# One output store of a mixture-of-experts kernel, put as five transfers in place of one

## The chip, the cores and the metric

The kernel runs on one core of a Trainium2 chip. The metric is the device time of one execution in microseconds (us). The core has a matrix engine (TensorE, PE in the profile), three engines that work on vectors (VectorE or DVE, ScalarE or ACT, GpSimd or POOL), a synchronisation engine (SyncE or SP) that here only issues transfers, and 16 DMA engines that all transfers between the chip's memory (HBM) and the core's on-chip memory (SBUF) share. A transfer is issued by GpSimd (queue q0 in the profile, called the ring here), by SP (q1) or by ScalarE (q10).

## The reference

Eight experts, each a two-layer network on its own 256 tokens:

```python
n_experts, capacity, hidden, expert_hidden = 8, 256, 512, 2048
h = np.matmul(x, w1) + b1[:, np.newaxis, :]
h = np.maximum(h, 0)
return (np.matmul(h, w2) + b2[:, np.newaxis, :]).astype(np.float32)
```

All inputs and the output are float32. The weights alone are 64 MB in HBM, the output is 4 MB.

## The kernel before

Tokens, hidden rows and expert rows are cut to the 128 partitions of SBUF. For each expert the weights are loaded by GpSimd, which converts them to fp16 on the way (`load_w1` L82, `load_w2` L88); x is loaded, for later experts in groups (`load_x` L72), and transposed in 32 x 32 blocks by VectorE (`transposes` L95). `first_product` (L114) makes relu(x w1 + b1) in PSUM and writes it as fp16 with ScalarE; `second_product` (L166) multiplies by w2, three experts later (LAG = 3), and calls `store`.

`store` (L142) copies the two halves of the result from PSUM to SBUF, one by VectorE (L156), one by ScalarE (L157). What follows depends on the expert. Experts 0 to 3 and experts 4 and 5 are groups (`GROUPS = {0: 4, 4: 2}`, L36): their results are gathered in one tile, 16 KB or 8 KB per partition, and only noted in `pending` when the last expert of the group is done. Expert 6 is stored at once in three parts (`PARTS`, L40): 25 rows by SP, 96 by ScalarE's queue, 7 by SP. Expert 7 is stored at once as 128 rows by SP (L164).

The order of GpSimd's transfers is written out by hand: `ring` (L215 to L225) is a list of (step, function, arguments), worked off from its head at the start of each step of the last loop (L227 to L234). The weights of the last experts come first, and then `flush` (L138) for the group of experts 0 to 3 and for the group of experts 4 and 5, so that these two stores, 2 MB and 1 MB, stand last in the ring. `ordered` keeps GpSimd's instructions in program order. The transfers of the ring signal on eight counters that are used in turn, and a transfer that takes a counter waits, where the program cannot tell it in another way, until the one before it on that counter has landed. At the end of the program SP waits for all counters, and a barrier over all engines closes it.

Of the kernel before, what the change touches and what calls it, by code (L numbers as in the profile page):

```python
# [10 lines left out]
def kernel(  # L11
# [9 lines left out]
    nc = tc.nc  # L21
# [16 lines left out]


    PARTS = {E - 2: ((0, 25, False), (25, 121, True), (121, 128, False))}  # L40
    nXF32 = 2
    X_LOADS = {2: 2, 4: 4}

    def ordered(ins):
        return tc.keep_in_program_order(ins)
# [91 lines left out]

    def flush(first):  # L138
        dst, src = pending.pop(first)
        ordered(nc.gpsimd.dma_start(out=dst, in_=src))  # L140

    def store(e, po):  # L142
        if e in group_of:
# [15 lines left out]
        if e in group_of:  # L159
            if e == first + n - 1:  # L160
                pending[first] = (dst, out_sb)
            return
        for p0, p1, scalar in PARTS.get(e, ((0, P, False),)):
            (nc.scalar if scalar else nc.sync).dma_start(out=dst[p0:p1], in_=out_sb[p0:p1])  # L164
# [23 lines left out]
    for e in range(nXF32):  # L188
# [4 lines left out]
        out=b2_sb,  # L193
        in_=b2.rearrange("e h -> (e h)").rearrange("(o f) -> o f", o=1),
# [12 lines left out]
    for b in range(nB):  # L207
        nc.vector.transpose(  # L208
            out=b1T[b * B : (b + 1) * B, nB - 1 - b : nB - 1 - b + nJ * B],
            in_=b1_rows.rearrange("r (i j) -> r j i", j=nJ),  # L210
# [13 lines left out]
    for first, n in GROUPS.items():  # L224
        ring.append((first + n + LAG, flush, (first,)))  # L225
# [40 lines left out]
```

## Time and profile before

| | |
|---|---|
| Time, median of 3 runs | 181.69 us (181.60 to 181.88) |
| Span of the profiled execution, first to last instruction | 179.7 us |
| DMA, read from and written to HBM | 71.39 MB and 4.19 MB, 421 GB/s over the span |
| PE busy (matrix products) | 129.1 us, 72% |
| DVE, ACT, POOL busy | 88.0, 70.2 and 13.1 us |
| Store of experts 0 to 3 (ring, 2 MB) | issued 148.26, 26.8 us to landing |
| Store of experts 4 and 5 (ring, 1 MB) | issued 159.71, 17.8 us to landing |
| Store of expert 7 (SP, 512 KB) | issued 173.94, 4.8 us to landing |

The profile is of one execution; times in it are counted from the start of its span, and no time of that execution beyond the span is given. A store lands when its last packet is confirmed. The trace has a record of every DMA packet with its start, duration, queue and size, but not with the DMA engine that moved it; a packet of 4 bytes is the one with which a DMA engine reports that its share of a transfer is done.

### The profile page before, as it was taken

How to read it: one execution, taken by the hardware profiler on the slowest of the kernel's cores; microseconds unless marked ns; L12 is line 12 of the kernel's file. 1: busy time of each engine (PE TensorE's matmuls, PEld its weight loads, DVE VectorE, ACT ScalarE, POOL GpSimd, SP SyncE). 2: the span in 40 equal slices, each digit the busy share in tenths (PEclk: the TensorE clock that was granted, in tenths of full speed). 3: DMA queues.
4: the chain of work that ended last, by engine and by line, in shares of the span. 5: the costliest groups of instructions: out<-in, count | busy, mean ns of one | idle time of the engine just before them, and what ended most of it. 6: DMA issues, size and time to landing. Idle time of an engine off the chain costs nothing.

```text
span 179.7 us, 1958 instructions
## 1 busy us (share of the span) xinstructions
PE 129.1 (72%) x784; PEld 85.8 (48%) x784; DVE 88.0 (49%) x125; ACT 70.2 (39%) x151; POOL 13.1 (7%) x28
## 2 busy tenths in 40 slices
PE   0005099969595970899969597969497887999950
PEld 0004079969592320795369244844195332433420
DVE  0999942987000199999999998003200020301010
ACT  0000459969593022483099005950586020020010
POOL 7000002120201010001010001000200021010000
PEclk9999999999998798589999889999999996999996
DMA  5999999999999999999999999999999999999996
GB/s 216 251 226 199 233 212 197 233 224 193 228 230 192 221 233 215 197 230 230 204 208 230 219 193 233 226 193 222 230 215 197 233 206 204 223 212 215 335 420 250
DMA packets 3829, 40.56 MB, mean 226 GB/s; under 512 B 461, under 2 KB 477, under 8 KB 1133
## 3 DMA queue, kind: packets, MB, share of 16 engines
q0 software_dynamic: 3232, 38.35, 96.6%
q1 hardware_dynamic: 476, 1.70, 2.4%
q10 hardware_dynamic: 112, 0.39, 0.5%
q8 instruction: 6, 0.10, 0.2%
q14 instruction: 3, 0.02, 0.0%
HBM read 71.39 MB, written 4.19 MB: 421 GB/s over the span
## 4 chain that ended last, share of the span: by engine, by line
DMA 66%; PE 26%; POOL 2%; another core or an unknown queue 1%; issue 1%; ACT 0%; POOLq 0%
DMA w1sb<-in_w_dram 44%; DMA w2sb<-in_w_dram 22%; PE po L178 18%; PE ph L121 8%; PE po L171 1%; POOL w1sb L84 1%; ACT out L157 0%; POOL x L76 0%; POOL b_sb L192 0%; POOL b_rows L196 0%; POOLq L250 0%
## 5 line engine op out<-in xcount | busy, mean ns | idle before, releaser
L121 PE MATMUL ph<-xT,w1sb 128*128 128x256 f16 x512 | 63.6, 289 | 34.8 <-DMA w1sb<-in_w_dram 23.9
L121 PEld LDWEIGHTS <-w1sb 128*128 128x128 f16 x512 | 59.0, 147 | 40.3 <-DMA w1sb<-in_w_dram 32.6
L178 PE MATMUL po<-w2sb,hT 128*128 128x512 f16 x256 | 61.4, 402 | 9.4 <-DMA w2sb<-in_w_dram 9.4
L112 DVE STREAM_TRANSPOSE xT<-x 32x256 f16<-32x256 f16 (+1 forms) x64 | 53.1, 889 | 25.6 <-DMA x<-in_x_dram 18.7
L128 ACT ACTIVATE hT<-ph,b1T 128x256 f16<-128x256 f32 x128 | 56.2, 474 | 13.6 <-PE ph L121 13.4
L178 PEld LDWEIGHTS <-hT 128*128 128x128 f16 x256 | 25.9, 102 | 44.7 <-issue 19.3
L156 DVE COPY out<-po 32x512 f32<-32x512 f32 (+2 forms) x22 | 15.1, 688 | 54.0 <-PE po L178 53.8
L157 ACT COPY out<-po 32x512 f32<-32x512 f32 (+2 forms) x22 | 12.7, 579 | 69.7 <-PE po L178 69.5
L109 DVE STREAM_TRANSPOSE xT<-x 32x256 f16<-32x256 f16 x32 | 14.0, 436 | 0.5
L93 POOL DMA_DIRECT2D w2sb<-in_w_dram x10 | 5.3, 534 | 72.8 <-PE po L178 72.8
L128 ACT ACT_TABLE_LOAD x1 | 1.3, 1283 | 20.5 <-DVE b1T L208 20.5
L84 POOL DMA_DIRECT2D w1sb<-in_w_dram x8 | 4.5, 558 | 63.2 <-PE ph L121 62.4
L171 PE MATMUL po<-b_sb,ones 1*128 1x512 f16 x16 | 4.8, 379 | 0.0
L208 DVE STREAM_TRANSPOSE b1T<-b_rows 32x512 f32<-32x512 f32 x4 | 4.1, 1035 | 0.1
L201 DVE CAST x<-x 128x1024 f16<-128x1024 f32 x2 | 1.5, 757 | 3.3 <-DMA x<-in_x_dram 3.3
L140 POOL DMA_DIRECT2D out_dram<-out x2 | 1.1, 542 | 10.9 <-ACT out L157 10.9
L171 PEld LDWEIGHTS <-ones 1*128 1x128 f16 x16 | 0.9, 92 | 2.1 <-issue 2.1
L76 POOL DMA_DIRECT2D x<-in_x_dram x2 | 1.1, 552 | 0.0
L197 DVE MEMSET ones<- 1x128 f16 x1 | 0.2, 165 | 0.8 <-PEq L250 0.8
L196 POOL DMA_DIRECT2D b_rows<-in_b_dram x1 | 0.5, 515 | 0.0
L192 POOL DMA_DIRECT2D b_sb<-in_b_dram x1 | 0.5, 513 | 0.0
L250 POOL MEMSET const-float32-0.0<- 128x1 f32 x1 | 0.1, 99 | 0.2 <-issue 0.2
(3 smaller groups left out, 0.3 us busy)
## 6 DMA issues: line engine op xcount, KB each, us to landing
w1sb<-in_w_dram POOLq DMA_DIRECT2D x8, 2048.0 KB, 34.5
w2sb<-in_w_dram POOLq DMA_DIRECT2D x6, 2048.0 KB, 46.8
w2sb<-in_w_dram POOLq DMA_DIRECT2D x4, 1024.0 KB, 24.0
out_dram<-out POOLq DMA_DIRECT2D x1, 2048.0 KB, 26.8
x<-in_x_dram SPq DMA_DIRECT2D x2, 512.0 KB, 3.9
x<-in_x_dram POOLq DMA_DIRECT2D x1, 1024.0 KB, 30.8
out_dram<-out POOLq DMA_DIRECT2D x1, 1024.0 KB, 17.8
x<-in_x_dram POOLq DMA_DIRECT2D x1, 512.0 KB, 24.0
```

The costliest lines, as they stand in the source:

```text
L84: ordered(nc.gpsimd.dma_start(out=w1_sb[e], in_=w1[e].rearrange("(p kc) m -> p kc m", kc=nKC)))
L93: ordered(nc.gpsimd.dma_start(out=w2_sb[e][:, lo : lo + half], in_=src[:, lo : lo + half]))
L109: nc.vector.transpose(out=out[:, :, g, :, 0, :], in_=block[:, :, :, 0, :])
L112: nc.vector.transpose(out=out[:, tb, g], in_=block[:, tb])
L121: ordered(nc.tensor.matmul(out=ph, lhsT=w1_sb[e][:, kc, :].rearrange("p (q j) -> p q j", j=nJ)[:, :, j], rhs=xT[e][:, kc, :], start=(kc == 0),
L128: nc.scalar.activation(out=hT[e][:, j, :].rearrange("p (tb k i) -> p tb k i", tb=nTB, k=split), in_=ph.rearrange("p (tb i k) -> p tb k i", ...
L156: nc.vector.tensor_copy(out=out_sb[at : at + rows, k * nTB, :], in_=po[0][part])
L157: nc.scalar.copy(out=out_sb[at : at + rows, k * nTB + 1, :], in_=po[1][part])
L171: ordered(nc.tensor.matmul(out=t, lhsT=ones1, rhs=b2_sb[0:1, e * H : (e + 1) * H], start=True, stop=False,))
L178: ordered(nc.tensor.matmul(out=po[tb], lhsT=hT[e][:, j, tb * P : (tb + 1) * P], rhs=w2_sb[e][:, j, :], start=False, stop=(j == nJ - 1),))
L201: nc.vector.tensor_copy(out=t, in_=x32[e])
L208: nc.vector.transpose(out=b1T[b * B : (b + 1) * B, nB - 1 - b : nB - 1 - b + nJ * B], in_=b1_rows.rearrange("r (i j) -> r j i", j=nJ),)
```

## The change

The store of experts 4 and 5 is a tile of 128 rows of 8 KB. Before, GpSimd puts it in the ring as one transfer. After, GpSimd puts the rows 0 to 65, 66 to 90, 91 to 101 and 102 to 126 as four transfers in this order, with the limit of 4096 bytes to a descriptor, so that a row is two runs of 4 KB; the last row, 127, is issued by SP, with a limit of 512.

```diff
     PARTS = {E - 2: ((0, 25, False), (25, 121, True), (121, 128, False))}
+    RING_PARTS = {4: ((0, 66), (66, 91), (91, 102), (102, 127))}
     nXF32 = 2
...
     def flush(first):
         dst, src = pending.pop(first)
-        ordered(nc.gpsimd.dma_start(out=dst, in_=src))
+        if first not in RING_PARTS:
+            ordered(nc.gpsimd.dma_start(out=dst, in_=src))
+            return
+        for p0, p1 in RING_PARTS[first]:
+            ordered(nc.gpsimd.dma_start(out=dst[p0:p1], in_=src[p0:p1], max_dma_last_dim=4096))
+        nc.sync.dma_start(out=dst[p1:], in_=src[p1:], max_dma_last_dim=512)
```

In the built program GpSimd has 30 instructions of note in place of 27, and SP 8 in place of 7: the one-row store stands after the two loads of x and before the stores of expert 6. The instructions of the other engines and their order are the same. The third and the fourth of the ring's parts wait for a counter of the ring each.

## The prediction, made before the run

> **What bounds the kernel now.** I read the slices of the span first (busy share of the 16 DMA engines in tenths, and what they moved), then the queues (packets, MB, share of 16 engines' time):
>
> ```profile
> DMA  5999999999999999999999999999999999999996
> GB/s 216 251 226 199 233 212 197 233 224 193 228 230 192 221 233 215 197 230 230 204 208 230 219 193 233 226 193 222 230 215 197 233 206 204 223 212 215 335 420 250
> ...
> q0 software_dynamic: 3232, 38.35, 96.6%
> q1 hardware_dynamic: 476, 1.70, 2.4%
> q10 hardware_dynamic: 112, 0.39, 0.5%
> q8 instruction: 6, 0.10, 0.2%
> ```
>
> The DMA engines are the bound from the first slice to the last; GpSimd's ring (q0) holds 96.6% of their time, SP's queue is q1, ScalarE's q10. In the last three slices only stores are left. The chain of waits (start, length, what) breaks off too early:
>
> ```profile
> 166.28 7.03 PE po L178 x32
> 173.31 0.02 issue
> 173.33 0.59 ACT out L157
> ```
>
> It ends at 173.92 us of 179.7, because nobody computes on what a store writes. So I read the store issues (KB, us to landing) and the end of the timeline (start, length, engine, line):
>
> ```profile
> out_dram<-out POOLq DMA_DIRECT2D x1, 2048.0 KB, 26.8
> ...
> out_dram<-out POOLq DMA_DIRECT2D x1, 1024.0 KB, 17.8
> ...
> out_dram<-out SPq DMA_DIRECT2D x1, 512.0 KB, 4.8
> ```
>
> ```profile
> 148.26 0.55 POOL L140 DMA_DIRECT2D out_dram<-out  x1
> 159.71 0.54 POOL L140 DMA_DIRECT2D out_dram<-out  x1 [10.90 <-ACT out L157]
> ```
>
> The changed store is the 1024 KB one, put in the ring at 159.71 and landed 17.8 us later, because loads and the 2 MB store are ahead of it. The last, expert 7's 512 KB by SP, is issued at 173.94 and lands at 178.78. The last 2 us, in half-microsecond windows (length, engines, clock, DMA share, GB/s):
>
> ```profile
> 177.00:177.50 0.50, 0.00 (x0) 0.00 (x0) 0.00 (x0) 0.00 (x0) 0.00 (x0) 0.50 0.93 377
> 177.50:178.00 0.50, 0.00 (x0) 0.00 (x0) 0.00 (x0) 0.00 (x0) 0.00 (x0) 0.50 0.70 287
> 178.00:178.50 0.50, 0.00 (x0) 0.00 (x0) 0.00 (x0) 0.00 (x0) 0.00 (x0) 0.50 0.27 107
> ```
>
> The share falls in steps: some engines are done a microsecond before others. The packet records (start, duration, queue, size) name no engine, but from 161.5 us on they lie end to end in exactly sixteen chains, none with a gap over 4 ns, each with 8 rows of each 128-row transfer. Five chains end at 177.04, 177.33, 177.38, 177.44 and 177.55; eleven at 178.07 to 178.43; the mean is 177.99. Five of the eleven, the SP chains from here on, are those that carry 5 rows each of SP's 25-row store; two more are the rest of the seven that its 7-row store used (25 rows left 5 completion packets, 7 rows left 7). The other four late ones carry no more rows than the early five. The q8 line says why they can be late: six instruction fetches of 16 KB, 0.9 to 1.0 us each, and six chains run about 1 us behind. The last packet, at 178.43, lands at 178.78, and SP's end waits and the closing barrier take until 179.7. A chain that ends late is the kernel's time, one for one.
>
> **The change part by part.** The sum is made against the profiled span, 179.7 us; the median of the runs is 181.69, 2.0 us more, which lies around the span and which I leave alone.
>
> *Issues on GpSimd.* Three more at 0.54 us: 1.6 us, so the four end at about 161.9 instead of 160.25. Nothing is queued behind them on GpSimd. Two carry new waits on ring counters whose transfers had landed by 149.50 and 154.42. The ring reaches this store at 173.02 at the earliest: 11 us of cover, cost nothing; without it, 1.6 us.
>
> *Order on SP.* The one-row store waits for expert 5's ScalarE copies (end 159.4) ahead of expert 6's stores, issued at 166.40. SP is idle in between, an issue takes 0.36 us: nothing. SP's end waits stay eight.
>
> *4 KB descriptors.* An 8 KB ring store packet starts 307 ns after the one before it, a 4 KB store packet on q1 and q10 155 ns (256 records). No ring store has 4 KB packets in this trace; I take 155. Two for one costs 3 ns per row, 0.03 us on a chain.
>
> *More pieces.* Each ends with a completion packet, 6 ns from start to start: three more are 0.02 us. [...] In this trace a chain goes from one ring transfer to the next within 10 ns, so the row decides.
>
> *Where the rows go.* This carries the sum, and the trace does not show it: all its ring transfers divide by sixteen. The nearest rows are SP's: 25 rows went to five engines, 5 each, 7 to seven, 1 each. By that, 66 rows are 11 engines x 6, 25 are 5 x 5, 11 are 11 x 1, 25 are 5 x 5. If each part starts where the one before stopped, sixteen engines are gone round twice: eleven get 7 rows, five get 10. If each starts at the first engine, as SP's two did, five get 17, six get 7, five none. I take the first: the instruction queue's fetches fell on six different chains, so a queue that moves on exists here; this is the weakest step. [...]
>
> With 7 rows a chain gets 14 x 155 + 18 - 8 x 307 = -0.27 us; with 10 rows 20 x 155 + 18 - 8 x 307 = +0.66 us. If the five are the early chains: 177.55 + 0.66 = 178.21, and the late 178.43 - 0.27 = 178.16. The end moves from 178.43 to 178.21: -0.22 us.
>
> *SP's one row.* The built program has it as one run of 2048 elements, while the ring parts show as rows of two 1024s: its limit of 512 has not cut it. One row on SP's queue goes by the row of 25 and 7 to one engine, and to one they also used: an SP chain, 0.31 us. Those end at 177.80 to 178.15 after the change; with the row at 178.11 to 178.46. Cut into sixteenths it costs each chain some 0.03 us, between a 4-byte and a 4 KB packet. So the end lies between 178.21 and 178.46, -0.22 to +0.03; over the five possible chains the mean is 178.34, which I take: -0.1 us. It also holds up one chain's loads by 0.31 us; those chains' loads land by 168.3, the slowest land at 169.23, and TensorE asks for them at 169.68.
>
> Forecast: 181.69 - 0.10 = **181.59 us**, own range 181.40 to 181.80 (-0.22 and +0.03, and the before runs' own scatter of 0.1 to 0.2).
>
> **The rivals.**
> 1. *The 25-row parts fall on late chains* (the ring's count starts elsewhere, or all sixteen are used with 10 rows on eleven). For: nothing in the trace ties the ring's order to the early five. Against: five and eleven are also the numbers of early and late chains. It decides as soon as one late chain takes 10 rows: 178.43 + 0.66 = 179.09; with SP's row on it 179.40; and if the ring's last landing is then the very last, SP has three more end waits of 0.06 behind it. +0.65 to +1.15: about 182.5 us, slower.
> 2. *Every part starts at the first engine.* SP's stores speak for it. Then an SP chain has 17 rows: 34 x 155 + 18 - 2456 = +2.83 us, 178.42 to 181.25: 184.5 us.
> 3. *The row on SP is spread after all, or falls on a light chain*, and the balance comes through whole: -0.2 us, 181.48. Against it stands the uncut run. The gain is capped: were all chains to end together, at the mean 177.99 plus 0.05, it would be 0.39 us, 181.30.
>
> A measurement of this kernel tells about 0.2% (0.36 us) from no change, so my own mechanism is mostly too small to be told.
>
> **How the numbers follow.** Forecast 0.42, rival 3 0.18, rival 1 0.32, rival 2 0.08. Faster by over 0.2% needs nearly the whole cap; most of that chance is in rival 3: 0.18. Within 0.2%: the forecast and the rest of rival 3, 0.42. Slower: rivals 1 and 2, 0.40. The range goes from 181.35 to 182.60: it takes in the forecast, most of rivals 3 and 1, and leaves out rival 2.
>
> **What would show it.** DMA share in the last half microseconds: above 0.9 until close to 178 and then a steep fall if balanced; if rival 1 holds, a longer low tail than now, with q0 packets past 177.2. The number of 4-byte packets on q0 and the chain each 25-row part stands on show the split; an 8192-byte q1 packet near 160 us shows SP's row uncut. If late chains do not end about 0.27 us earlier, the split is wrong; if they do and the end stays, SP's row or a wait behind the ring's landing holds it.

## The result, and the profile after

The changed kernel takes 183.08 us (median of 6 runs, 182.53 to 183.54); the kernel before took 181.73 us beside it (6 runs, 181.50 to 182.01). The ratio is 1.0075, 95% interval 1.0060 to 1.0089: slower by 0.75%, 1.35 us between the medians. Medians and ratios here and below are of fast runs; one run of all, 272.43 us in e3, was slow and stands in neither. The profiled execution after took 182.94 us, its span is 181.1 us against 179.7.

The slices of the span of the changed kernel (busy share of the 16 DMA engines in tenths, and what they moved), then its queues:

```profile
DMA  6998999999899989998999999999999999999994
GB/s 231 232 232 190 232 232 203 206 226 232 186 228 201 248 192 224 228 217 192 232 224 213 199 232 224 210 203 232 224 206 206 228 201 210 226 208 210 403 371 166
...
q0 software_dynamic: 3696, 38.34, 96.3%
q1 hardware_dynamic: 478, 1.71, 2.5%
```

Up to the last three slices both kernels move 186 to 251 GB/s in every slice. In those three it was 335, 420 and 250 GB/s before and is 403, 371 and 166 now. (The slices are 4.5 us long and no longer begin at the same moments, so only their run is compared.) The ring's queue has 464 packets more.

The chain of waits of the changed kernel (start, length, what) ends where it ended before, 0.3 us later, and the store of expert 7 follows it:

```profile
169.98 3.63 PE po L184 x16
173.63 0.59 ACT out L163
```

The issues of stores (KB, us to landing) and the line of the issues in the timeline (start, length):

```profile
out_dram<-out POOLq DMA_DIRECT2D x1, 2048.0 KB, 27.4
...
out_dram<-out POOLq DMA_DIRECT2D x1, 528.0 KB, 19.8
...
out_dram<-out SPq DMA_DIRECT2D x1, 512.0 KB, 6.0
out_dram<-out POOLq DMA_DIRECT2D x2, 200.0 KB, 19.2
...
out_dram<-out POOLq DMA_DIRECT2D x1, 88.0 KB, 19.4
```

```profile
158.14 2.59 POOL L145 DMA_DIRECT2D out_dram<-out  x4 [9.31 <-ACT out L163]
```

The four issues take 2.59 us in all. The ring's parts land about 19 to 20 us after they were issued, and the store of expert 7, which the change does not touch, now takes 6.0 us in place of 4.8.

The end in windows (start to end, length, five engines, clock, share of the DMA engines' time, GB/s), before and then after:

```profile
174.00:177.00 3.00, 0.00 (x0) 0.00 (x0) 0.00 (x0) 0.00 (x0) 0.00 (x0) 0.95 0.96 401
177.00:178.00 1.00, 0.00 (x0) 0.00 (x0) 0.00 (x0) 0.00 (x0) 0.00 (x0) 0.50 0.81 332
178.00:179.00 1.00, 0.00 (x0) 0.00 (x0) 0.00 (x0) 0.00 (x0) 0.00 (x0) 0.50 0.14 53
```

```profile
174.00:177.00 3.00, 0.00 (x0) 0.00 (x0) 0.00 (x0) 0.21 (x1) 0.00 (x0) 1.00 0.99 342
177.00:178.00 1.00, 0.00 (x0) 0.00 (x0) 0.00 (x0) 0.00 (x0) 0.00 (x0) 1.00 0.90 275
178.00:179.00 1.00, 0.00 (x0) 0.00 (x0) 0.00 (x0) 0.00 (x0) 0.00 (x0) 1.00 0.77 299
179.00:180.00 1.00, 0.00 (x0) 0.00 (x0) 0.00 (x0) 0.00 (x0) 0.00 (x0) 0.50 0.17 70
```

This is the reading that matters. From 174 to 177 us the share went up, from 0.96 to 0.99, and the rate went down, from 401 to 342 GB/s. The engines are not idle for want of work, and work that is badly dealt out would not lower the rate at a full share: packets take longer. The packet records say so too. Before, all 128 packets of this store took 309 to 318 ns. After, 37 of its 254 ring packets of 4 KB took over 175 ns where the others took 159, up to 899 ns, 8.6 us too much in all. SP's 4 KB packets of expert 7's store have lost 0.8 us and the last 16 KB ones 1.2 us beside them. So 10.6 us of engine time, 0.66 us on each of 16 engines, went into slow packets, plus 290 packets of 4 bytes, 9 ns each for most and 7 for some (2.6 us at 9 ns, 0.16 us on each). The mean end of the sixteen chains rose from 177.99 to 179.00 us, so that these two make 0.8 of the 1.0 us; the rest is open.

That the store of expert 7 was issued 0.3 us later is not the cause: among the runs below, e12 issued it at 174.06 us and lost nothing, and e4 at 173.65, the earliest of all, and is among the slowest.

### The profile page after: what moved, and what is told of

It is laid out like the page before. It is cut to its first block, busy times and chain, and to the rows that moved or that the text cites. A ratio compares the mean times of both kernels' runs of the same rounds, so it can differ in the third digit from the quotient of the medians.

```text
span 181.1 us, 1963 instructions
## 1 busy us (share of the span) xinstructions
PE 126.6 (70%) x784; PEld 86.0 (47%) x784; DVE 87.9 (49%) x125; ACT 70.5 (39%) x151; POOL 15.3 (8%) x31
## 4 chain that ended last, share of the span: by engine, by line
DMA 60%; PE 19%; DVE 9%; issue 6%; ACT 1%; POOL 0%; another core or an unknown queue 0%; POOLq 0%; ACTq 0%
DMA w1sb<-in_w_dram 46%; PE ph L122 13%; DMA w2sb<-in_w_dram 12%; PE po L184 6%; DVE xT L110 6%; DVE b1T L214 2%; DMA x<-in_x_dram 2%; DVE x L207 1%; ACT L129 1%; ACT out L163 0%; PE po L177 0%; ACT hT L129 0%; POOL w2sb L94 0%; POOLq L85 0%
## 5 line engine op out<-in xcount | busy, mean ns | idle before, releaser
L122 PE MATMUL ph<-xT,w1sb 128*128 128x256 f16 x512 | 65.8, 296 | 38.6 <-DMA w1sb<-in_w_dram 27.0
L122 PEld LDWEIGHTS <-w1sb 128*128 128x128 f16 x512 | 60.4, 148 | 44.9 <-DMA w1sb<-in_w_dram 37.2
L184 PE MATMUL po<-w2sb,hT 128*128 128x512 f16 x256 | 56.7, 379 | 8.3 <-DMA w2sb<-in_w_dram 8.3
L184 PEld LDWEIGHTS <-hT 128*128 128x128 f16 x256 | 24.7, 98 | 40.1 <-issue 11.9
L145 POOL DMA_DIRECT2D out_dram<-out x4 | 2.6, 652 | 9.3 <-ACT out L163 9.3
L142 POOL DMA_DIRECT2D out_dram<-out x1 | 0.5, 543 | 0.0
```

The costliest lines, as they stand in the source:

```text
L122: ordered(nc.tensor.matmul(out=ph, lhsT=w1_sb[e][:, kc, :].rearrange("p (q j) -> p q j", j=nJ)[:, :, j], rhs=xT[e][:, kc, :], start=(kc == 0),
L184: ordered(nc.tensor.matmul(out=po[tb], lhsT=hT[e][:, j, tb * P : (tb + 1) * P], rhs=w2_sb[e][:, j, :], start=False, stop=(j == nJ - 1),))
```

## The experiments

Two theories stood first. By the *place* theory the rows of the new parts lie on the wrong engines: late chains take 10 rows, and packets go at their normal pace. By the *crowding* theory something in the new transfers slows the packets: their 4 KB size, their number, the packets of 4 bytes, or the stretch of partitions that each covers. Every run changes only this store, unless said otherwise. The table gives the median, the ratio to the kernel before on the same chip, and the packets of this store in the ring that took over a tenth more than their nominal 159 ns (4 KB) or 309 ns (8 KB), with the time that these lost in all. The code below is shortened to the lines that matter (`...` marks a gap).

| run | store of experts 4 and 5 | median us | ratio, 95% interval | slow packets | lost us |
|---|---|---|---|---|---|
| e1_again | as changed | 183.29 (one run) | | 48 of 254 | 10.2 |
| e2_shift2 | as changed, another load cut | 184.39 | 1.0148 (1.0106 to 1.0190) | 24 of 254 | 7.2 |
| e3_neutral | 55, 25, 48 rows, 4 KB | 184.08 | 1.0123 (1.0100 to 1.0147) | 64 of 256 | 16.9 |
| e4_k16 | 48, 32, 16, 32 rows, 4 KB | 184.33 | 1.0151 (1.0129 to 1.0174) | 95 of 256 | 23.8 |
| e5_one4k | 128 rows at once, 4 KB | 181.62 | 1.0000 (0.9980 to 1.0019) | 0 of 256 | 0 |
| e6_no4k | as changed, 8 KB | 184.38 | 1.0149 (1.0131 to 1.0168) | 36 of 127 | 16.8 |
| e7_halves | 64 and 64 rows, 8 KB | 183.92 | 1.0124 (1.0106 to 1.0142) | 38 of 128 | 13.4 |
| e8_cols | 128 rows, columns in halves | 181.63 | 1.0002 (0.9980 to 1.0024) | 0 of 256 | 0 |
| e9_shift_true | as changed, another load cut | 184.68 | 1.0165 (1.0134 to 1.0196) | 54 of 254 | 14.2 |
| e10_sbuf_half | two transfers from 64 partitions each, all over HBM | 183.51 | 1.0096 (1.0078 to 1.0113) | 76 of 256 | 11.9 |
| e11_hbm_half | two transfers from 128 partitions, HBM in two blocks | 181.82 | 1.0009 (0.9997 to 1.0021) | 0 of 256 | 0 |
| e12_every_other | 64 even rows, 64 odd rows, 8 KB | 181.65 | 1.0003 (0.9980 to 1.0026) | 0 of 128 | 0 |

**The change once more, and with its place shifted.** The first is the changed kernel itself. The second cuts an early load of 32 rows, so that the ring's count of engines should begin elsewhere. The *divisor rule* of the expectations is the author's estimate from SP's stores of before, where 25 rows went to five engines and 7 to seven: a part goes to as many engines as the largest number up to 16 that divides its rows.

```diff
-    ordered(nc.gpsimd.dma_start(out=b1_rows, in_=b1.rearrange("e (b i) -> (e b) i", b=nB)))
+    b1_src = b1.rearrange("e (b i) -> (e b) i", b=nB)
+    for p0, p1 in ((0, 28), (28, 32)):
+        ordered(nc.gpsimd.dma_start(out=b1_rows[p0:p1], in_=b1_src[p0:p1]))   # e2; e9 adds max_dma_last_dim=1024
```

> The changed kernel once more, for a second profile. Three terms are under suspicion for its +1.4 us. Place: the ring's 25-row parts (10 rows per engine) stand on five engines of which two are among the six late ones, +0.66 us. Bursts: an engine that has no row of a part gets as many 4-byte packets as the others get data packets (290 in all), and data packets beside such bursts are slow, +0.8 us. Pieces: 4 KB descriptors and four transfers cost more in themselves. If the starting engine of the ring's count is fixed, this profile shows again three early and two late chains with 4-byte packets at the place of the 66-row part, and about 183.0 us. If the count is left over from what ran before, another number of late chains, and a time between 181.5 and 183.5.

> The changed kernel, with the load of b1 put as 28 and 4 rows in place of 32, which by the divisor rule moves the ring's count on by 14 + 4 = 18, two engines past where it was. Place: if the count starts anew in each execution, the 25-row parts now stand on the five early chains, and the time falls by about 0.66 us, to some 182.4 (to 181.6 if place is all). If the count is carried over, it moves on by two in each execution and the times spread over 181.6 to 183.5. Bursts and pieces: no gain from the shift, 183.0 to 183.2.

The first gave 183.29 us and 48 slow packets: the crowding belongs to the change, not to one execution. The second gave 184.39 us, above what either theory had (183.5 at most), and the 66-row part ended early on the same classes of engines as in the changed kernel, three early chains and two later ones. Whether the count was shifted can't be told from that, and the run does not separate the theories. Its ring lands at 180.84 us, later than in the changed kernel (179.17), with fewer slow packets; why is open.

**The same number of rows for each engine.** By the divisor rule 55 rows are 11 engines x 5, 25 are 5 x 5 and 48 are 16 x 3, so every engine gets 8 rows as before. The second run uses only multiples of 16. Neither has SP's row.

```diff
-    RING_PARTS = {4: ((0, 66), (66, 91), (91, 102), (102, 127))}
+    RING_PARTS = {4: ((0, 55), (55, 80), (80, 128))}             # e3
+    RING_PARTS = {4: ((0, 48), (48, 80), (80, 96), (96, 128))}   # e4
```

> The ring store as 55, 25 and 48 rows in 4 KB descriptors, no row by SP: every engine gets 5 + 3 rows again, wherever the count starts, but 160 of the 4-byte packets stay. Place: as before, 181.7 to 181.8. Bursts: about half of 0.8 us, 182.0 to 182.5. Pieces: about 182.5 to 183.

> The ring store as 48, 32, 16 and 32 rows in 4 KB descriptors, no row by SP: four pieces and 4 KB as in the changed kernel, but all divide by sixteen, so no 4-byte packets beyond the completions and 8 rows on each engine. Place and bursts: as before, 181.7 to 181.9. Pieces: 183.0.

Both are slower than the changed kernel, 1.0123 and 1.0151, with no row misplaced by that rule, and slower than any theory had them (183.0 at most). The ring's packets fit the rule in e3: 3552 are before's 3232, 128 more of data, 32 completions and 160 of 4 bytes for engines without a share. The windows of e3 and of e4:

```profile
174.00:177.00 3.00, 0.00 (x0) 0.00 (x0) 0.00 (x0) 0.00 (x0) 0.00 (x0) 0.76 1.00 307
```

```profile
174.00:177.00 3.00, 0.00 (x0) 0.00 (x0) 0.00 (x0) 0.00 (x0) 0.00 (x0) 0.67 0.90 238
177.00:178.00 1.00, 0.00 (x0) 0.00 (x0) 0.00 (x0) 0.00 (x0) 0.00 (x0) 0.50 0.95 283
178.00:179.00 1.00, 0.00 (x0) 0.00 (x0) 0.00 (x0) 0.00 (x0) 0.00 (x0) 0.50 0.77 213
179.00:180.00 1.00, 0.00 (x0) 0.00 (x0) 0.00 (x0) 0.00 (x0) 0.00 (x0) 0.50 0.49 172
```

The engines' share is 1.00 and 0.90, and they move 307 and 238 GB/s where they moved 401 before. The queue's line of e4 shows that it has none of the extra packets of 4 bytes (3408 is before's 3232, 128 more data packets and three more parts of 16 completions):

```profile
q0 software_dynamic: 3408, 38.35, 95.7%
```

The place theory falls as the main cause, and so do the packets of 4 bytes. Left are the 4 KB size (*Descriptors* in the expectations), the number of parts, and the stretch of partitions that a part covers (*Partitions*).

**Size and number apart.** One transfer with 4 KB descriptors; the changed kernel without them; two parts of 64 rows; two halves of the columns.

```diff
# e5, against the kernel before
+        ordered(nc.gpsimd.dma_start(out=dst, in_=src, **({"max_dma_last_dim": 4096} if first == 4 else {})))
...
# e6, against the changed kernel
-            ordered(nc.gpsimd.dma_start(out=dst[p0:p1], in_=src[p0:p1], max_dma_last_dim=4096))
+            ordered(nc.gpsimd.dma_start(out=dst[p0:p1], in_=src[p0:p1]))
...
# e7, against the kernel before
+        for p0, p1 in ((0, 64), (64, 128)) if first == 4 else ((0, 128),):
+            ordered(nc.gpsimd.dma_start(out=dst[p0:p1], in_=src[p0:p1]))
...
# e8, against the kernel before
+        step = src.shape[1] // 2 if first == 4 else src.shape[1]
+        for r0 in range(0, src.shape[1], step):
+            ordered(nc.gpsimd.dma_start(out=dst[:, r0 : r0 + step], in_=src[:, r0 : r0 + step]))
```

> The store of experts 4 and 5 as one transfer of 128 rows again, but in 4 KB descriptors. The store in four pieces that divide by sixteen cost 2.7 us, with its 4 KB packets far over 159 ns, so misplaced rows and 4-byte packets are not the main cause. [...] Descriptors: 4 KB packets out of the ring are slow in themselves: 183.5 to 184.5 here. [...]

> The changed kernel (66, 25, 11 and 25 rows, the last by SP) without the limit of 4 KB, so one descriptor of 8 KB to a row. Descriptors: back to 181.5 to 182.2. Partitions: slow as the changed kernel, 182.5 to 183.5, with 8 KB packets over 309 ns.

> Two transfers of 64 rows in 8 KB descriptors, four rows to an engine each, no row by SP. Descriptors: as before, 181.6 to 181.9. [...]

> Two transfers over all 128 rows, each of half of the columns: 4 KB packets and two pieces, but every partition in each. Descriptors: 183.5 to 184.5. Partitions: as before, 181.6 to 181.9.

One transfer of 4 KB descriptors costs nothing: 1.0000, all its 256 packets at 159 ns, and its windows are those of before:

```profile
174.00:177.00 3.00, 0.00 (x0) 0.00 (x0) 0.00 (x0) 0.00 (x0) 0.00 (x0) 0.85 1.00 410
177.00:178.00 1.00, 0.00 (x0) 0.00 (x0) 0.00 (x0) 0.00 (x0) 0.00 (x0) 0.50 0.75 307
```

Two halves by columns cost nothing either (1.0002). Two halves by rows, with 8 KB packets and an equal number of rows for each engine, cost 1.24%:

```profile
174.00:177.00 3.00, 0.00 (x0) 0.00 (x0) 0.00 (x0) 0.02 (x1) 0.00 (x0) 0.86 0.99 358
177.00:178.00 1.00, 0.00 (x0) 0.00 (x0) 0.00 (x0) 0.00 (x0) 0.00 (x0) 0.50 1.01 250
178.00:179.00 1.00, 0.00 (x0) 0.00 (x0) 0.00 (x0) 0.00 (x0) 0.00 (x0) 0.50 0.58 172
```

From 177 to 178 us every engine is busy (the modelled share is 1.01) at 250 GB/s. 38 of the 128 packets are slow, 12 of them 560 to 680 ns, about twice 309, one 1333 ns. So it is neither the size nor the number: it is the stretch of rows. The run without the 4 KB descriptors is slow too (1.0149, 184.38 us, above the 183.5 expected) but tells less, because its split is another: its queue has 33 extra packets of 4 bytes in place of 290, which is what comes out if each part goes to all sixteen engines with the count rounded up, 10 rows on eleven of them, the second way that rival 1 names.

```profile
q0 software_dynamic: 3312, 38.34, 95.5%
```

**Which memory it is, and whether place adds to it.** A stretch of 64 rows is a stretch of 64 partitions on the chip, and a block of 512 KB in HBM. e10 reads 64 partitions and writes all over HBM, e11 reads all partitions and writes one block, both with 4 KB packets. In both the rows of experts 4 and 5 land at other places of the output, so they serve for the time alone. e9 repeats the shift with two descriptors for each row of the load.

```diff
# e10, for the group of experts 4 and 5
+        for k in range(2):
+            to = dst[:, 2 * k : 2 * k + 2].rearrange("(a b) r h -> a b r h", b=2)
+            at = src[64 * k : 64 * k + 64].rearrange("p (b r) h -> p b r h", b=2)
+            ordered(nc.gpsimd.dma_start(out=to, in_=at))
...
# e11, the same with
+            to = dst[64 * k : 64 * k + 64].rearrange("p (b r) h -> (p b) r h", b=2)
+            at = src[:, 2 * k : 2 * k + 2]
```

> The changed kernel with b1 loaded as 28 and 4 rows in two descriptors each. The shift of the run before with 28 and 4 rows did not take place (the 66-row part again landed at once on three early and two late engines); rows of one descriptor seem to be shared out over all sixteen engines, rows of two by the divisor. Place: now all five early engines land the 66-row part at once, and the two late chains lose their three extra rows: about 0.66 us less than the changed kernel, 182.3 to 182.6. If the ring's count is carried from one execution to the next, the times spread instead. If only partitions matter, 183.0 to 183.3.

> Two transfers, each from 64 of the 128 partitions, but written to HBM in 4 KB runs spread over the whole 1 MB, as the column halves were (the rows of experts 4 and 5 land in another order). If the crowding is on the side of the on-chip memory: slow as the row halves, 183.3 to 184. If it is in HBM, which the row halves wrote in two blocks of 512 KB: 181.6 to 181.9, packets of 159 ns.

> The other way round: two transfers from all 128 partitions, half of the columns each, written to HBM as two blocks of 512 KB (the rows of experts 4 and 5 land in another order). On-chip memory: 181.6 to 181.9. HBM: 183.3 to 184.

The first window of e10 and of e11:

```profile
174.00:177.00 3.00, 0.00 (x0) 0.00 (x0) 0.00 (x0) 0.00 (x0) 0.00 (x0) 0.82 0.96 324
```

```profile
174.00:177.00 3.00, 0.00 (x0) 0.00 (x0) 0.00 (x0) 0.00 (x1) 0.00 (x0) 1.00 0.96 395
```

Half the partitions: 324 GB/s and 1.0096. Half the HBM rows: 395 GB/s and 1.0009, no slow packet. It is the on-chip side. The shift in e9 again left the 66-row part early on three early and two later chains (174.45, 174.55, 174.57 and 175.75, 175.81 us), and it took 184.68 us, so its expectation was missed, and what the place of the rows is worth by itself stays open.

**64 rows that are not a stretch.** The same as the halves, with the even rows and then the odd ones:

```diff
+        step = 2 if first == 4 else 1
+        for k in range(step):
+            ordered(nc.gpsimd.dma_start(out=dst[k::step], in_=src[k::step]))
```

> Two transfers of 64 rows in 8 KB descriptors as the row halves, but the even rows first and then the odd ones, so each transfer reaches from the first partition to the last. If what crowds is the stretch of partitions that a transfer covers: faster than the row halves (183.9), 181.7 to 183.0. If any transfer of fewer than 128 partitions crowds, whichever they are: 183.5 to 184.3.

```profile
174.00:177.00 3.00, 0.00 (x0) 0.00 (x0) 0.00 (x0) 0.04 (x1) 0.00 (x0) 1.00 0.99 412
177.00:178.00 1.00, 0.00 (x0) 0.00 (x0) 0.00 (x0) 0.00 (x0) 0.00 (x0) 0.82 0.78 320
```

412 GB/s, 1.0003, the longest packet 327 ns. Two transfers of 64 rows cost nothing when the rows lie over all partitions, and 1.24% when each is a stretch. That settles the cause here: the ring's transfers that each covered only a stretch of partitions were served more slowly, packet by packet (38 slow packets of 128 in e7, 76 of 256 in e10), and those whose rows lay over all partitions were not (0 of 128 in e12).

The trace of before sets a limit to this. SP's store of the rows 0 to 24 of expert 6 is a stretch too, but on five engines, and its packets took 159 to 162 ns, those of SP's other stores included. So a stretch of 25 rows on five engines was not slow there, and the halves of e7, four rows to an engine on all sixteen, were. And in the same trace ScalarE's store of the rows 25 to 120 on sixteen engines, other rows than those of a store of all 128, took 159 ns in all 96 packets, so that a stretch of 96 rows was not slow either, and an engine need not have the rows that it has in a full store. How short a stretch has to be, and on how many engines, was not tried.

What makes the packets of a stretch slow, no run shows: the stretch is what is shown. The halves cost 1.0124 x 181.56 - 181.56 = 2.25 us (2.36 between the medians), and the rate fell from 401 GB/s before to 358 from 174 to 177 us, and from 332 to 250 from 177 to 178; another store, that of expert 7, runs beside it.

## Why the prediction was wrong

Forecast were 181.59 us, range 181.35 to 182.60; measured 183.08. Its chance for slower was 0.40, and rival 1 (182.5) came nearest in time; what its own reason, late chains with 10 rows, was worth, no run shows. Step by step:

- **What bounds the kernel**: right. The DMA engines' last chain is the time: its end moved from 178.43 to 179.92 us, by 1.49, and the span by 1.4.
- **Issues on GpSimd**: four at 0.55 to 0.72 us, 2.59 in all, over by 160.72. Nothing waits for them: right (the ring's first packet of this store started at 173.18 us before, not at 173.02, and at 173.54 after). So was **order on SP**: expert 7's store is held by ScalarE's copy, as before.
- **4 KB descriptors at 155 ns**: right for a transfer over all partitions (159 ns each, ratio 1.0000), wrong for this one: 193 ns in the mean over 254. The q1 and q10 rows it was taken from were of stores that ran without slow packets.
- **More pieces: "a chain goes from one ring transfer to the next within 10 ns, so the row decides"**: this is the step that failed. The row is right, and shows only that transfers over all 128 partitions follow one another within 10 ns. It does not show what a part of the partitions costs, and the trace of before has no ring store that covers a part of them. What a stretch costs a packet was put at nothing. The loss is not between the transfers, the packets within them are slow: from 170 us on the packets of after, too, lie in sixteen chains, with no gap over 52 ns, and its 4 KB ring packets took 193 ns in the mean in place of 159. Missing from the sum is this term: +0.66 us for slow packets on the mean chain, and 0.16 for packets of 4 bytes.
- **Where the rows go**: the split was right, five engines with 10 rows and eleven with 7. The 464 extra packets of the ring are 126 of data, 48 completions and 290 of 4 bytes, and 290 is just what the divisor rule gives if each engine without a share gets as many 4-byte packets as another has data packets (66 rows: 5 x 12, 25: 11 x 10, 11: 5 x 2, 25: 11 x 10). **"If the five are the early chains"** was half wrong. The 66-row part was over at once on three early engines (174.53 to 174.67) and about 1 us later on two others (175.55, 175.89); these five have no rows of it, so they are the ones with 10 rows later. Rival 1's condition, a late chain with 10 rows, was met by two. Its 179.09 us for their end plus 0.8 us, if they lost as much by slow packets and 4-byte packets as the mean chain, is 179.9, and the last two chains end at 179.88 and 179.92, the next at 179.59. This sum fits, but that these are the two was not established, the place term was not separated by a run, and e3 and e4 show that the crowding alone is enough to make the kernel slower.
- **SP's one row**: right. One packet of 8192 bytes at 161.93 us, uncut, with one completion. The last weights landed at 169.93 us in place of 169.23, and TensorE waited for them, which the prediction did not have; but in e8 they landed at 169.80 and nothing was lost.
- **The gain by balance**: not only lost but turned round: the last chain was 0.44 us behind the mean before and is 0.92 behind it after.
- **What would show it**: the share in the last half microseconds did stay high and fall late, as the prediction wanted it of a balanced end. From 177.0 to 177.5 it was 0.96 against 0.93. But the rate beside it was 238 GB/s against 377. The test looked at the wrong column:

```profile
177.00:177.50 0.50, 0.00 (x0) 0.00 (x0) 0.00 (x0) 0.00 (x0) 0.00 (x0) 1.00 0.96 238
```

## What to carry to other kernels

Cut a store by columns or by every second row, which cost nothing here (1.0002, 1.0003), and not, in the ring, by stretches of partitions such as these, of 11 to 66 rows, which cost 0.75 to 1.5% here, where the DMA engines were the bound (1.65% with another load cut beside it). Read the DMA share together with the GB/s beside it: a high share at a falling rate was slow packets here (0.99 at 342 GB/s, against 0.96 at 401 before), and eight rows on every engine did not mend that (e4, 1.0151). Before rows are moved between engines for balance, work out the cap (0.39 us here) and ask whether the trace has a transfer of the new shape at all.

## What the runs showed beside it

GpSimd's closing drain ends 1.0 to 1.2 us after the ring's last landing. Its line in the source view, before and then after (duration ns, shortest, median and longest; first and last start):

```profile
L261 POOLq DRAIN  x3: 45/93/18881, 159.7 to 179.4; - x3
```

```profile
L267 POOLq DRAIN  x3: 40/93/20649, 159.7 to 180.9; - x3
```

The longest, from 159.7 us, ends at 178.57 before, where the ring's last landing is at 177.54, and at 180.33 after, with the landing at 179.17. SP's own last waits end at 178.92 and 180.39, 0.15 us after SP's last landing. So a landing of the ring counted about 0.9 to 1.1 us more than a landing of SP's: before, the ring had 0.36 us of cover left at the end, after, 0.06. In e2 and e9 the ring landed at 180.84 and the drain ended at 182.04 and 182.03; there it, and not SP's landings (180.65, 181.46), sets the span of 182.8 us. Why the ring lands that late in those two is open.

Rows of one descriptor and rows of two seem to have been dealt out in different ways: the same parts left 33 extra packets of 4 bytes with 8 KB descriptors (e6), 290 with 4 KB. And the 4-byte packets were not free: 7 to 9 ns each.
